# A two-layer network kernel whose instruction order is planned once, or planned in four passes ranked by latest begin

## The chip, the cores and the metric

The kernel runs on one core of one Trainium2 chip. The core has a matrix engine (TensorE, PE in the profile, with its weight loads as PEld), three engines for elementwise work (VectorE, DVE; ScalarE, ACT; GpSimd, POOL) and SyncE (SP), whose queue issues every transfer between device memory and the on-chip memory. The metric is the device time of one execution in microseconds (us). Each engine takes its instructions in the order in which the program lists them: an instruction that waits holds up all that stand behind it on its engine.

## The reference

All data are float32; x is 1024 tokens by 1024 features.

```python
for layer in range(2):
    h = rmsnorm(x, mix_norm[layer])
    # layer 0: sliding-window attention; layer 1: HGRN2 recurrence
    y = attention(h, ...) if layer % 2 == 0 else hgrn2(h, ...)
    x = x + y
    h = rmsnorm(x, mlp_norm[layer])
    x = x + square(relu(h @ w_up)) @ w_down          # 1024 -> 4096 -> 1024
return rmsnorm(x, final_norm)

def attention(h):    # 16 query heads, 4 key heads of 64, blocks of 128, window 128
    q, k, v = split(h @ w_qkv + b_qkv); q, k = rotary(q), rotary(k)
    scores = (q @ k.T) / 8, masked to the window, with a sink per head
    return (softmax with sink)(scores) @ v @ w_o

def hgrn2(h):        # 8 heads of 128, chunks of 64 tokens
    q, f, i, g = split(h @ w_in, 4)
    forget = lb + (1 - lb) * sigmoid(f); k = 1 - forget
    state = forget * state + outer(k, i); o = silu(q) @ state
    return (rmsnorm(o, g_norm) * silu(g)) @ w_o
```

## The kernel before

**Arithmetic.** Every float32 operand of a large product is split into a high part, rounded to the matrix engine's fast float32 form, and a low part, the remainder. A product is then three matmuls: high by high, high by low, low by high. For a weight block of 128x512 the high part is a cast (a tile named wh, on ACT or DVE) and the low part a subtraction on DVE (wl). The square products are done by Strassen's scheme, so weights and activations are also added and subtracted on DVE (tiles m and t) before they are split. The names after the letter are numbers of tiles: wr is a raw weight block as it is loaded, a and t are activations, sm are small columns of statistics, p and q are banks of PSUM, the matrix engine's accumulators (four of each), d are spills to device memory.

**Stages.** The tokens are worked in two halves of 512. In the profile the attention layer takes about 0 to 330 us, the first MLP 330 to 900, the recurrence 900 to 1400, the second MLP 1400 to 2070, the final norm the rest.

**What sets the order.** Nothing is issued when the model code runs. Each operation is recorded as an `Op` with the engines that may take it, a cost for each, and the tiles that it reads and writes (`Schedule.add`). Then `Schedule.order()` plays the whole list against a cost model: five engines, a latency from each engine to each other (`LATENCY`), a tail of 2750 ns behind every transfer, a `DRAIN` of 200 ns where the matmuls change between whole and column form, and for each sort of tile so many buffers (60 of a, 18 of t, 6 each of m and wr, 5 each of wh and wl, 4 each of p and q). Whenever an engine is free it takes, of the operations that are ready, the one of lowest rank. The rank is the place in the recorded program, less 100 for weight work (`LEAD`) and for what reads a p bank (`EVACUATE`). Buffers of a sort are given out in the order in which the program first uses them. `issue()` then emits the operations in the order found, so every instruction has the one line L337, that of the helper `issue` in `Net.call`, in the profile.

**What else is told apart there.** `copy` (casts and copies) and `square_relu` may go to ACT or DVE, and `better_elsewhere` decides by the waiting work of both. All loads and stores go through `dma` on SP.

Of the kernel before, what the change touches and what calls it, by code (L numbers as in the profile page):

```python
# [82 lines left out]
class Buf:  # L83
    def __init__(self, pool, bufs, shape, dtype, tag, name):
        self.pool, self.bufs, self.shape, self.dtype, self.tag, self.name = pool, bufs, shape, dtype, tag, name
        self.tile = None
        self.writer, self.readers = {}, {}
        self.uses, self.users = 0, []
        self.freed = 0.0
# [32 lines left out]
class Op:  # L122
    __slots__ = ("ways", "tail", "bufs", "first", "wait", "ready", "after", "rank", "engine", "form")
# [11 lines left out]
DRAIN = {"whole": 200.0, "columns": 200.0}  # L135
FULL = {512: 227.3, 256: 119.8}
# [6 lines left out]
class Schedule:  # L143
# [8 lines left out]
    def add(self, ways, outs, ins, tail=0.0, form=None):  # L152

        op = Op()
        op.ways, op.tail, op.engine, op.form = ways, tail, None, form
# [3 lines left out]
        op.rank, op.ready, op.after, op.first = (len(self.ops) - lead, len(self.ops)), 0.0, [], []  # L162
# [11 lines left out]
        op.bufs = list(bufs)  # L174
# [6 lines left out]
        op.wait = len(before) + len(op.bufs)  # L181
        for o in before:
            o.after.append(op)
        self.ops.append(op)

    def order(self):
        free_at, pending, ready, done, form = {}, {}, {}, [], None
        slots, queue = {}, {}
        for key, bufs in self.tags.items():
            slots[key] = [(0.0, k) for k in range(bufs[0].bufs)]  # L190
            queue[key] = list(reversed(bufs))

# [7 lines left out]
        def give(key):  # L200
            while queue[key] and slots[key]:
                b = queue[key].pop()
                t, b.slot = heapq.heappop(slots[key])
                for op in b.users:
                    met(op, t)

        for op in self.ops:
# [3 lines left out]
        for key in self.tags:  # L211
            give(key)
        def better_elsewhere(op, e, t):
# [8 lines left out]
        while True:  # L222
# [60 lines left out]
class Net:  # L283
# [48 lines left out]
    def op(self, engine, fn, outs, ins, cost, *args, tail=0.0, form=None, **kw):  # L332
        self.s.add({engine: self.call(fn, *args, **kw) + (cost,)}, outs, ins, tail, form)
# [13 lines left out]
    def dma(self, out, in_, nbytes):  # L347
        self.op("SP", self.nc.sync.dma_start, [out], [in_], max(450.0, nbytes / 320.0), out, in_, tail=2750.0)
# [7 lines left out]
    def act(self, out, in_, func, n=TH, bias=None, scale=1.0, accum=None):  # L356
# [6 lines left out]
        if accum is not None:  # L363
# [3 lines left out]
                out, in_, func, scale=scale, **kw)  # L367
# [1288 lines left out]
```

## Time and profile before

| what | value |
|---|---|
| median of 3 runs | 2086.56 us (2084.07 to 2086.97) |
| the profiled execution | 2086.78 us, of which the span from first to last instruction is 2084.9 us |
| mean granted TensorE clock | 0.997 |
| PE busy | 2062.8 us, 99% |
| DVE busy | 1893.6 us, 91% |
| ACT busy | 1122.4 us, 54% |
| transfers | 407.43 MB, mean 195 GB/s |

The busy time of PE comes from modelled ends, so two matmuls in a row may overlap in it. What the table leaves of PE, 2084.9 - 2062.8 = 22.1 us, is the time in which no matmul was under way. The rows that place these microseconds stand in the prediction.

### The profile page before, as it was taken

To read this page: it belongs to the slowest core of one execution; us is meant where nothing else is said; L and a number is where in the kernel's file an instruction comes from. 1 tells how busy PE (TensorE), PEld (TensorE's weight loads), DVE (VectorE), ACT (ScalarE), POOL (GpSimd) and SP (SyncE) were. 2 spreads that over 40 slices of the span, in tenths; PEclk is the share of its full clock that TensorE was granted. 3 is DMA by queue.
4 is the path that set the end of the run, shared out by engine and by line. 5 is a ranking of instruction groups with operands and counts; after the bars stand their busy time and mean duration, and the time that the engine had idled before them with its cause. 6 is when DMAs were issued, how large, how long until landed. Compare 5 with 4: busy or idle time off the path is not lost.

```text
span 2084.9 us, 35687 instructions
## 1 busy us (share of the span) xinstructions
PE 2062.8 (99%) x12220; PEld 1741.4 (84%) x12220; DVE 1893.6 (91%) x3919; ACT 1122.4 (54%) x2280; POOL 59.8 (3%) x121
## 2 busy tenths in 40 slices
PE   9999999999999999999999999999999999999998
PEld 7778888888898888887888888888788888888887
DVE  8889899999999989989898888888999999998995
ACT  5566777655565424556444444452765556432453
POOL 4030000000000000000000000000000000000000
PEclk9999999999999999999999999999999999999999
DMA  6212277867679967632222222567786768986732
GB/s 221 79 51 80 83 243 265 279 224 247 225 256 317 324 196 254 225 137 77 98 96 101 102 98 90 209 228 233 262 284 231 244 229 269 311 308 208 249 103 81
DMA packets 225845, 407.43 MB, mean 195 GB/s; under 512 B 25344, under 2 KB 30464, under 8 KB 225664
## 3 DMA queue, kind: packets, MB, share of 16 engines
q1 hardware_dynamic: 225664, 405.16, 57.1%
q8 instruction: 96, 1.57, 0.3%
q14 instruction: 85, 0.70, 0.1%
HBM read 321.17 MB, written 83.89 MB: 194 GB/s over the span
## 4 chain that ended last, share of the span: by engine, by line
PE 90%; DVE 5%; issue 2%; ACT 1%; DMA 1%; SPq 0%; POOLq 0%; POOL 0%; DVEq 0%; ACTq 0%
PE p L337 47%; PE q L337 43%; DVE t L337 2%; DVE a L337 2%; DVE wl L337 1%; ACT a L337 1%; DMA a<-d 0%; DVE m L337 0%; DMA a<-in_x 0%; ACT t L337 0%; DMA wr<-in_up 0%; ACT wh L337 0%; SPq L337 0%; ACT m L337 0%; DMA wr<-in_wo 0%
## 5 line engine op out<-in xcount | busy, mean ns | idle before, releaser
L337 PE MATMUL p<-a,wh 128*128 128x512 f32 (+1 forms) x2880 | 809.9, 365 | 0.8 <-ACT t L337 0.8
L337 PE MATMUL q<-a,wh 128*128 128x512 f32 x2112 | 655.0, 391 | 2.0 <-ACT t L337 1.9
L337 PEld LDWEIGHTS p<-a,wh 128*128 128x128 f32 x2880 | 514.5, 189 | 85.9 <-ACT t L337 2.1
L337 PE MATMUL p<-a,wl 128*128 128x512 f32 (+1 forms) x1440 | 520.7, 362 | 0.3 <-DVE wl L337 0.3
L337 PEld LDWEIGHTS q<-a,wh 128*128 128x128 f32 x2112 | 390.2, 188 | 79.0 <-ACT t L337 3.4
L337 PE MATMUL q<-a,wl 128*128 128x512 f32 x1056 | 410.9, 390 | 1.0 <-DVE wl L337 1.0
L337 PEld LDWEIGHTS p<-a,wl 128*128 128x128 f32 x1440 | 271.5, 189 | 40.7 <-DVE wl L337 0.8
L337 DVE TENSOR_TENSOR wl<-wr,wh 128x512 fp32r<-128x512 f32 x352 | 243.0, 692 | 7.9 <-ACT wh L337 3.3
L337 DVE TENSOR_TENSOR wl<-m,wh 128x512 fp32r<-128x512 f32 x338 | 232.0, 692 | 7.3
L337 ACT CAST wh<-wr 128x512 fp32r<-128x512 f32 x249 | 154.0, 619 | 150.5 <-PE p L337 107.2
L337 PEld LDWEIGHTS q<-a,wl 128*128 128x128 f32 x1056 | 198.7, 188 | 43.1 <-DVE wl L337 1.4
L337 ACT ACTIVATE t<-t 128x512 f32<-128x512 f32 x254 | 159.8, 632 | 111.2 <-DVE t L337 105.2
L337 ACT CAST wh<-m 128x512 fp32r<-128x512 f32 x240 | 149.1, 622 | 124.1 <-PE q L337 60.4
L337 DVE TENSOR_TENSOR a<-t,a 128x512 fp32r<-128x512 f32 (+2 forms) x314 | 208.4, 686 | 0.3 <-ACT t L337 0.3
L337 DVE TENSOR_TENSOR t<-t,t 128x512 f32<-128x512 f32 (+3 forms) x337 | 199.0, 607 | 3.7 <-ACT t L337 2.6
L337 ACT CAST a<-t 128x512 fp32r<-128x512 f32 (+1 forms) x212 | 127.0, 613 | 132.8 <-PE q L337 85.2
L337 ACT COPY t<-q 128x512 f32<-128x512 f32 (+2 forms) x201 | 112.5, 560 | 107.4 <-PE q L337 96.9
L337 PE MATMUL p<-wh,a 128*128 128x512 f32 x384 | 124.5, 396 | 1.1 <-DVE wl L337 1.1
L337 DVE TENSOR_TENSOR m<-wr,wr 128x512 f32<-128x512 f32 (+1 forms) x188 | 122.0, 652 | 2.5 <-DMA wr<-in_down 1.6
L337 DVE TENSOR_TENSOR t<-t,p 128x256 f32<-128x256 f32 x294 | 117.8, 420 | 0.0
L337 PEld LDWEIGHTS q<-t,t 128*64 128x64 f32 (+1 forms) x2160 | 95.5, 144 | 13.2 <-issue 7.3
L337 PE MATMUL q<-t,t 128*64 128x32 f32 (+2 forms) x2160 | 104.6, 229 | 0.0
(129 smaller groups left out, 2397.6 us busy)
## 6 DMA issues: line engine op xcount, KB each, us to landing
t<-d SPq DMA_DIRECT2D x548, 256.0 KB, 4.3
d<-t SPq DMA_DIRECT2D x244, 256.0 KB, 2.8
wr<-in_down SPq DMA_DIRECT2D x224, 256.0 KB, 4.2
wr<-in_up SPq DMA_DIRECT2D x178, 256.0 KB, 3.8
wr<-in_win SPq DMA_DIRECT2D x68, 256.0 KB, 2.6
a<-d SPq DMA_DIRECT2D x60, 256.0 KB, 4.5
wr<-in_wqkv SPq DMA_DIRECT2D x48, 256.0 KB, 2.6
d<-a SPq DMA_DIRECT2D x48, 256.0 KB, 3.8
```

The costliest lines, as they stand in the source:

```text
L337: fn(*[place(a) for a in args], **{k: place(v) for k, v in kw.items()})
```

## The change

The plan is made four times. `forward()` is the old `order()`, with a dearer cost model: loads have a tail of 3000 ns and stores of 2000, a change of the function table on ACT (Sqrt, Sin, Exp or Tanh after another) is charged 1283 ns, and ACT and DVE may not read one PSUM bank at the same time. Behind each plan `backward()` walks it from its end: for every operation it finds the latest begin that would still let everything behind it keep its time, given the engine it was put on and the buffers it was given. PE's operations stay in the planned order there and get no later than planned. In the next pass the rank of every operation that isn't PE's is this latest begin; PE's operations keep their program rank. The buffers of a sort are given out in the order of their first use in the plan just made. Of the four plans the one that ends first by the cost model is issued.

```diff
+LOAD, STORE = 3000.0, 2000.0
+READERS = {"ACT": "DVE", "DVE": "ACT"}
+TABLES = {AF.Sqrt: "sqrt", AF.Sin: "sin", AF.Exp: "exp", AF.Tanh: "exp"}
+TABLE, REUSE, PASSES = 1283.0, 200.0, 4
...
-    def order(self):
-        free_at, pending, ready, done, form = {}, {}, {}, [], None
+    def forward(self):
+
+        free_at, pending, ready, done, form, table = {}, {}, {}, [], None, None
...
         for key, bufs in self.tags.items():
-            slots[key] = [(0.0, k) for k in range(bufs[0].bufs)]
+            slots[key] = [(0.0, k, None) for k in range(bufs[0].bufs)]
             queue[key] = list(reversed(bufs))
+            for b in bufs:
+                b.uses, b.freed, b.read = len(b.users), 0.0, {}
...
+            if e in READERS:
+                held = max((b.read.get(READERS[e], 0.0) for b in op.banks), default=0.0)
+                if held > t + 1.0:
+                    heapq.heappush(p, (held, op.rank, op))
+                    continue
             op.engine, cost = e, op.ways[e][1]
+            for b in op.banks:
+                b.read[e] = t + cost + 130.0
             if op.form and op.form != form:
                 form, t = op.form, t + DRAIN[op.form]
-            free_at[e] = t + cost
-            end = t + cost + op.tail
+            if op.table and op.table != table:
+                table, t = op.table, t + TABLE
+            op.begin, free_at[e] = t, t + cost
+            op.end = end = t + cost + op.tail
...
-                    heapq.heappush(slots[key], (b.freed + 200.0, b.slot))
+                    heapq.heappush(slots[key], (b.freed + REUSE, b.slot, b))
...
+    def backward(self, done):
+        end = max(op.end for op in done)
+        place, heaps, free_at = {}, {e: [] for e in ENGINES}, dict.fromkeys(ENGINES, end)
+        for k, op in enumerate(done):
+            place[op], op.then, op.wait, op.late = k, [], 0, end
+        last = None
+        for op in done:
+            for o in op.before:
+                o.then.append((op, LATENCY[o.engine][op.engine]))
+            for b in op.first:
+                if b.previous:
+                    for o in b.previous.users:
+                        o.then.append((op, REUSE))
+            if op.engine == "PE":
+                if last:
+                    last.then.append((op, 0.0))
+                last = op
+        behind = {op: [] for op in done}
+        for op in done:
+            op.wait = len(op.then)
+            for o, gap in op.then:
+                behind[o].append((op, gap))
+        def push(op):
+            heapq.heappush(heaps[op.engine], (-op.late, -place[op], op))
+        for op in done:
+            if op.wait == 0:
+                push(op)
+        while any(heaps.values()):
+            e = max((e for e in ENGINES if heaps[e]), key=lambda e: min(free_at[e], heaps[e][0][2].late - heaps[e][0][2].tail))
+            _, _, op = heapq.heappop(heaps[e])
+            op.late = min(free_at[e], op.late - op.tail) - op.ways[e][1]
+            if e == "PE":
+                op.late = min(op.late, op.begin)
+            free_at[e] = op.late
+            for o, gap in behind[op]:
+                o.late = min(o.late, op.late - gap)
+                o.wait -= 1
+                if o.wait == 0:
+                    push(o)
+        for op in done:
+            if op.engine != "PE":
+                op.rank = (op.late, op.index)
+        for bufs in self.tags.values():
+            bufs.sort(key=lambda b: min(place[op] for op in b.users))
+    def order(self):
+        best = None
+        for k in range(PASSES):
+            done = self.forward()
+            end = max(op.end for op in done)
+            if best is None or end < best[0]:
+                best = (end, [(op, op.engine) for op in done], [(b, b.slot) for bufs in self.tags.values() for b in bufs])
+            self.backward(done)
+        for op, engine in best[1]:
+            op.engine = engine
+        for b, slot in best[2]:
+            b.slot = slot
+        return [op for op, _ in best[1]]
...
-        self.op("SP", self.nc.sync.dma_start, [out], [in_], max(450.0, nbytes / 320.0), out, in_, tail=2750.0)
+        self.op("SP", self.nc.sync.dma_start, [out], [in_], max(450.0, nbytes / 320.0), out, in_, tail=LOAD if isinstance(out, View) and out.buf.tag[0] != "d" else STORE)
...
-                out, in_, func, scale=scale, **kw)
+                out, in_, func, scale=scale, table=TABLES.get(func), **kw)
```

The recorded operations and the tiles are the same, and so is the number of instructions (10862 on PE, 1562 transfers). Only their order moves, and by the choice between ACT and DVE 6 casts and 5 of the squared relus go from ACT to DVE, all of 128x512. 9060 of PE's 10862 instructions stand at the same place as before. The helper's line is L416 in the changed program.

**VectorE in the attention layer (79 to 88 us in the trace of before).** a242 to a252 are query columns after the rotary step, which the first score products read. sm238 to sm240 are a norm's mean square, its root (which ACT makes) and the inverse root. Before:

```order
L337 TENSOR_SCALAR sm238_1154<-q237_1083 128x4
L337 SCALAR_TENSOR_TENSOR a242_1100<-q241_1090,a242_1100 64x512
L337 TENSOR_TENSOR a202_1092<-t203_1139,t204_1146 128x8x8
L337 RECIPROCAL sm239_1159<-sm239_1159 128x4
L337 SCALAR_TENSOR_TENSOR a243_1112<-q241_1090,a243_1112 64x512
L337 TENSOR_TENSOR sm240_1175<-sm239_1159 128x4
L337 SCALAR_TENSOR_TENSOR a245_1123<-q244_1097,a245_1123 64x512
L337 SCALAR_TENSOR_TENSOR sm240_1175<-sm238_1154,sm240_1175 128x4
L337 SCALAR_TENSOR_TENSOR a246_1132<-q244_1097,a246_1132 64x512
L337 SCALAR_TENSOR_TENSOR sm239_1159<-sm240_1175,sm239_1159 128x4
L337 SCALAR_TENSOR_TENSOR a248_1141<-q247_1106,a248_1141 64x512
L337 SCALAR_TENSOR_TENSOR a249_1149<-q247_1106,a249_1149 64x512
```
and now:

```order
L416 SCALAR_TENSOR_TENSOR a242_1100<-q241_1090,a242_1100 64x512
L416 SCALAR_TENSOR_TENSOR a243_1112<-q241_1090,a243_1112 64x512
L416 TENSOR_TENSOR a193_1069<-t194_1118,t195_1125 128x8x8
L416 SCALAR_TENSOR_TENSOR a245_1121<-q244_1097,a245_1121 64x512
L416 SCALAR_TENSOR_TENSOR a248_1132<-q247_1108,a248_1132 64x512
L416 SCALAR_TENSOR_TENSOR a246_1138<-q244_1097,a246_1138 64x512
L416 SCALAR_TENSOR_TENSOR a249_1142<-q247_1108,a249_1142 64x512
L416 SCALAR_TENSOR_TENSOR a251_1151<-q250_1115,a251_1151 64x512
L416 SCALAR_TENSOR_TENSOR a252_1157<-q250_1115,a252_1157 64x512
L416 COPY_PREDICATED m255_811<-c6364_68,c6566_71 128x2x128
L416 RECIPROCAL sm239_1163<-sm239_1163 128x4
L416 TENSOR_TENSOR wl307_1189<-wr305_998,wh306_1177 128x512
```
The RECIPROCAL, which needs the root from ACT, stood ahead of all but one of the query columns; now they all stand ahead of it.

**VectorE at the begin of the first MLP (338 to 345 us).** The t1021 rows are a running sum of squares, read by the column product q1029; m, wh and wl are weights of Strassen's scheme. Before:

```order
L337 TENSOR_TENSOR t1021_4097<-t1021_4097,t1023_4111 128x512
L337 TENSOR_TENSOR m1072_4363<-m1071_4342,wr1067_4100 128x512
L337 TENSOR_TENSOR t1021_4097<-t1021_4097,t1024_4176 128x512
L337 TENSOR_TENSOR m1073_4375<-wr1067_4100,wr1069_4158 128x512
L337 TENSOR_TENSOR t1021_4097<-t1021_4097,t1025_4205 128x512
L337 TENSOR_TENSOR m1074_4388<-wr1068_4132,m1072_4363 128x512
L337 TENSOR_TENSOR t1021_4097<-t1021_4097,t1026_4232 128x512
L337 TENSOR_TENSOR wl1076_4400<-m1071_4342,wh1075_4351 128x512
L337 TENSOR_TENSOR t1021_4097<-t1021_4097,t1027_4271 128x512
L337 TENSOR_TENSOR wl1078_4410<-m1072_4363,wh1077_4371 128x512
L337 TENSOR_TENSOR t1021_4097<-t1021_4097,t1028_4279 128x512
L337 TENSOR_TENSOR wl1080_4425<-m1074_4388,wh1079_4394 128x512
```
and now:

```order
L416 TENSOR_TENSOR t1017_3958<-t1017_3958,t970_3773 128x512
L416 TENSOR_TENSOR wl1056_4301<-m1047_4116,wh1055_4261 128x512
L416 TENSOR_TENSOR m1072_4310<-m1071_4256,wr1067_4122 128x512
L416 TENSOR_TENSOR t1021_4015<-t1021_4015,t1026_4119 128x512
L416 TENSOR_TENSOR a1002_4320<-t965_3849,a1001_4275 128x512
L416 TENSOR_TENSOR a1004_4328<-t969_3903,a1003_4299 128x512
L416 TENSOR_TENSOR t1021_4015<-t1021_4015,t1027_4184 128x512
L416 TENSOR_TENSOR t1013_3905<-t1013_3905,t966_3766 128x512
L416 TENSOR_TENSOR t1021_4015<-t1021_4015,t1028_4205 128x512
L416 TENSOR_TENSOR wl1058_4354<-wr1044_4079,wh1057_4291 128x512
L416 TENSOR_TENSOR a1011_4367<-t1009_3816,a1010_4103 128x512
L416 TENSOR_TENSOR wl1078_4372<-m1072_4310,wh1077_4356 128x512
```
The last sum (of t1028) stood behind wl1078 and now stands three rows ahead of it; m1073, m1074, wl1076 and wl1080, which stood around wl1078, have gone behind it, and it stands nine rows sooner (row 710, was 719).

**TensorE at the same place (344 us).** Before:

```order
L337 MATMUL q943_4150<-a1003_4290,wl1056_4295 128x512
L337 MATMUL q953_4221<-a989_3977,wh1077_4371 128x512
L337 MATMUL q953_4221<-a990_3993,wh1077_4371 128x512
L337 MATMUL q953_4221<-a989_3977,wl1078_4410 128x512
L337 MATMUL q953_4221<-a991_4053,wh1077_4371 128x512
L337 MATMUL q943_4150<-a1006_4140,wh1057_4297 128x512
L337 MATMUL q1029_4428<-c23_69,t1021_4097 128x1 x4
L337 MATMUL q943_4150<-a1007_4263,wh1057_4297 128x512
```
and now:

```order
L416 MATMUL q943_4159<-a1004_4328,wh1055_4261 128x512
L416 MATMUL q943_4159<-a1003_4299,wl1056_4301 128x512
L416 MATMUL q1085_4422<-a959_3822,wh1075_4325 128x512
L416 MATMUL q1085_4422<-a960_3853,wh1075_4325 128x512
L416 MATMUL q1085_4422<-a959_3822,wl1076_4392 128x512
L416 MATMUL q1085_4422<-a963_3841,wh1075_4325 128x512
L416 MATMUL q1085_4422<-a964_3859,wh1075_4325 128x512
L416 MATMUL q1085_4422<-a963_3841,wl1076_4392 128x512
```
The first product with wl1078 was row 1483; now q1085, which reads wl1076, stands there, and wl1078 is first read 25 rows later, at row 1508.

**ScalarE at 1472 to 1478 us, in the second MLP.** COPY t4199 empties bank q4198. In before 15 rows lie between it and COPY t4094, of which the last eleven stand here:

```order
L337 CAST a4142_17615<-t4108_17253 128x512
L337 ACTIVATE t4161_17623<-a4015_17145 128x512
L337 ACTIVATE t4163_17628<-a4035_17244 128x512
L337 CAST a4145_17634<-t4144_17437 128x512
L337 ACTIVATE t4164_17640<-a4045_17296 128x512
L337 ACTIVATE t4165_17646<-a4055_17361 128x512
L337 ACTIVATE t4166_17652<-a4065_17424 128x512
L337 CAST a4136_17657<-t4096_17111 128x512
L337 CAST a4149_17664<-t4148_17487 128x512
L337 ACTIVATE t4167_17671<-a4075_17490 128x512
L337 CAST wh4196_17676<-wr4183_17406 128x512
L337 COPY t4199_17682<-q4198_17611 128x512
```
Now, from COPY t4094 on:

```order
L416 COPY t4094_17616<-q4092_17552 128x512
L416 ACTIVATE t4084_17525<-t4084_17525 128x512 x2
L416 CAST wh4196_17632<-wr4183_17409 128x512
L416 ACTIVATE t4167_17641<-a4075_17501 128x512
L416 CAST wh4214_17658<-m4210_17650 128x512
L416 COPY t4199_17663<-q4198_17626 128x512
L416 CAST a4149_17672<-t4148_17380 128x512
```
Four rows (five instructions) are left between the two copies; most of the squares of a (t4160 to t4166) and the casts that stood there went ahead of the first copy or behind the second.

More of the change, by code (lines that the diff above doesn't have):

```diff
@@ L88, in __init__ @@
         self.uses, self.users = 0, []
[L89 removed]
+        self.freed, self.previous, self.read = 0.0, None, {}
     def keys(self, part):
@@ L122 @@
 class Op:
-    __slots__ = ("ways", "tail", "bufs", "first", "wait", "ready", "after", "rank", "engine", "form")
+    __slots__ = ("ways", "tail", "bufs", "first", "before", "after", "banks", "table", "rank", "form", "index",
+                 "wait", "ready", "engine", "begin", "end", "late", "then")
 ENGINES = ("SP", "PE", "ACT", "DVE", "Pool")
@@ L150, in tile, with add @@
         return View(Buf(pool, bufs, shape, dtype, tag, name))
-    def add(self, ways, outs, ins, tail=0.0, form=None):
+    def add(self, ways, outs, ins, tail=0.0, form=None, table=None):
         op = Op()
-        op.ways, op.tail, op.engine, op.form = ways, tail, None, form
+        op.ways, op.tail, op.form, op.table, op.index = ways, tail, form, table, len(self.ops)
         lead = self.lead
@@ L161, in add @@
             lead = max(lead, EVACUATE)
-        op.rank, op.ready, op.after, op.first = (len(self.ops) - lead, len(self.ops)), 0.0, [], []
+        op.rank, op.after, op.first = (len(self.ops) - lead, len(self.ops)), [], []
         before, bufs = set(), {}
@@ L173, in add @@
         before.discard(op)
-        op.bufs = list(bufs)
+        op.bufs, op.before = list(bufs), list(before)
+        op.banks = [v.buf for v in ins if isinstance(v, View) and v.buf.tag in "pq"]
         for b in op.bufs:
@@ L202, in give @@
                 b = queue[key].pop()
-                t, b.slot = heapq.heappop(slots[key])
+                t, b.slot, b.previous = heapq.heappop(slots[key])
                 for op in b.users:
                     met(op, t)
+        for op in self.ops:
+            op.wait, op.ready, op.engine = len(op.before) + len(op.bufs), 0.0, None
         for op in self.ops:
@@ L329, in psum, with op @@
         return self.tile(tag, BUFS[tag], (P, TH), F32, self.pp)
-    def op(self, engine, fn, outs, ins, cost, *args, tail=0.0, form=None, **kw):
-        self.s.add({engine: self.call(fn, *args, **kw) + (cost,)}, outs, ins, tail, form)
+    def op(self, engine, fn, outs, ins, cost, *args, tail=0.0, form=None, table=None, **kw):
+        self.s.add({engine: self.call(fn, *args, **kw) + (cost,)}, outs, ins, tail, form, table)
     def call(self, fn, *args, **kw):
```

1 line of the change is left out of this document (removed).

## The prediction

> **What bounds the kernel now.** I read the page's busy line first, then the stretches, then for whom TensorE waits, last the rows around each wait.
>
> ```profile
> PE 2062.8 (99%) x12220; PEld 1741.4 (84%) x12220; DVE 1893.6 (91%) x3919; ACT 1122.4 (54%) x2280; POOL 59.8 (3%) x121
> ```
>
> TensorE carries the time: 2062.8 of the span of 2084.9 us. The matmuls stay the same, so a new order can give back only what TensorE waits, at most 22.1 us. Where these are (window, its length, then busy us of PE, PEld, DVE, ACT, POOL, the granted clock, DMA share, GB/s):
>
> ```profile
> 0.00:100.00 100.00, 94.49 (x447) 77.48 (x448) 86.88 (x239) 56.91 (x125) 24.66 (x50) 1.00 0.45 153
> 100.00:200.00 100.00, 97.81 (x569) 76.33 (x567) 91.35 (x222) 64.06 (x209) 19.09 (x38) 1.00 0.17 59
> 200.00:300.00 100.00, 99.99 (x595) 79.84 (x594) 91.76 (x185) 74.74 (x239) 3.61 (x10) 1.00 0.43 146
> 300.00:400.00 100.00, 98.90 (x477) 82.77 (x476) 97.02 (x198) 69.78 (x126) 0.00 (x0) 0.98 0.80 271
> 340.00:350.00 10.00, 9.00 (x37) 7.12 (x36) 9.81 (x22) 3.51 (x7) 0.00 (x0) 0.83 0.80 269
> 400.00:900.00 500.00, 500.00 (x2583) 429.59 (x2582) 465.02 (x879) 261.30 (x445) 0.36 (x2) 1.00 0.74 250
> 900.00:1000.00 100.00, 98.82 (x600) 80.69 (x600) 93.80 (x208) 54.08 (x104) 0.54 (x2) 1.00 0.27 93
> 1000.00:1400.00 400.00, 398.62 (x3451) 334.99 (x3449) 349.55 (x801) 191.80 (x421) 7.70 (x17) 1.00 0.37 127
> 1400.00:1500.00 100.00, 98.14 (x447) 81.10 (x446) 91.87 (x178) 47.70 (x87) 0.00 (x0) 1.00 0.76 253
> 1500.00:2000.00 500.00, 500.00 (x2624) 431.06 (x2623) 469.61 (x904) 264.61 (x453) 0.00 (x0) 1.00 0.77 259
> 2000.00:2085.00 85.00, 76.01 (x447) 67.54 (x445) 56.79 (x116) 37.42 (x77) 3.86 (x3) 0.95 0.14 52
> ```
>
> The MLPs (400 to 900, 1500 to 2000) lose nothing, the last 85 us 8.99 and the first 100 us 5.51. In between lie the places that an order can mend: 2.19 us in 100 to 200, 1.10 in 300 to 400, 1.18 in 900 to 1000, 1.38 from there to 1400, 1.86 to 1500. VectorE is the only other engine near full. TensorE's largest waits (total us, times, longest):
>
> ```profile
> PE q L337 <- ACT t L337: 3.4, 4, 1.3
> PE q L337 <- DVE a L337: 2.6, 5, 1.6
> PE q L337 <- DVE t L337: 2.6, 4, 0.9
> PE p L337 <- DVE wl L337: 1.8, 3, 1.1
> ```
>
> They are for ACT and DVE, whose order the change replaces.
>
> **The change part by part.** The sum is made against the profiled execution, 2086.78 us, of which 1.9 lie around the span; it stands 0.22 above the median of 2086.56.
>
> *Attention.* TensorE's rows, then VectorE's, then ScalarE's:
>
> ```profile
> 40.11 0.44 PE L337 MATMUL q<-c,t 128*128 128x128 f32 x2 [0.85 <-DVE t L337]
> ...
> 83.09 0.35 PE L337 MATMUL q<-a,a 128*128 128x256 f32 x1 [1.56 <-DVE a L337]
> ```
> ```profile
> 82.04 0.18 DVE L337 RECIPROCAL sm<-sm 128x4 f32<-128x4 f32 x1 [1.85 <-ACT sm L337]
> 82.25 0.69 DVE L337 SCALAR_TENSOR_TENSOR a<-q,a 64x512 fp32r<-64x512 f32 x1
> ```
> ```profile
> 80.51 1.28 ACT L337 ACT_TABLE_LOAD   x1
> 81.80 0.20 ACT L337 ACTIVATE sm<-sm 128x4 f32<-128x4 f32 x1
> ```
>
> The RECIPROCAL heads VectorE's queue and waits 1.85 us for the root, which ScalarE makes behind a table load of 1.28. Behind it waits the row at 82.25 (a243); 0.15 us after that ends, TensorE goes on with the first score product. The new plan charges the table load and puts all query rows ahead of the RECIPROCAL. Late next: that product also moves eight rows forward on TensorE (319, was 327), some 8 x 0.23 = 1.8 us, so the wait goes only if a243 comes 1.56 + 1.8 = 3.4 us sooner. It stands sixteen rows sooner on VectorE, but part of what it passed is soon wanted too. I take -1.0 of 1.56 (0 to -1.56). At 40.11 the transposes wait 0.85 for t121; its last DVE row is 18 sooner (97, was 115), TensorE's 17 (123, was 140): -0.5 (0 to -0.85). From 100 to 200 the waits are many and short: -1.0 of 2.19 (0 to -2.19). The start (5.51 less 0.85 and 1.56 is 3.1 us) is the first loads: 0.
>
> *First MLP's begin.*
>
> ```profile
> 344.53 0.50 PE L337 MATMUL q<-a,wl 128*128 128x512 f32 x1 [1.00 <-DVE wl L337]
> ...
> 346.13 0.72 PE L337 MATMUL q<-a,wh 128*128 128x512 f32 x1
> ...
> 349.63 0.62 PE L337 MATMUL q<-a,wh 128*128 128x512 f32 x2
> 350.09 0.40 PE L337 MATMUL q<-a,wl 128*128 128x512 f32 x1
> ```
> ```profile
> 343.77 0.70 DVE L337 TENSOR_TENSOR wl<-m,wh 128x512 fp32r<-128x512 f32 x1
> 344.37 0.70 DVE L337 TENSOR_TENSOR t<-t,t 128x512 f32<-128x512 f32 x1
> ```
>
> TensorE waits 1.00 us for wl1078, made at 343.77 among sums that nobody reads before 345. Soon after it runs slow: the 8 matmuls from 346.13 to 349.63 take 0.437 us each, the two from 349.63 to 350.09 0.23; the window 340 to 350 has a clock of 0.83. That is 8 x 0.207 = 1.66 us, 2.66 with the wait. In the new order wl1078 stands nine rows sooner, 9 x 0.60 = 5.4 us by the step of these two rows, and is read 25 rows later. Late next is wl1076, now read in its place (row 1484, was 1500) and only three rows sooner on VectorE. I take -2.2 (0 to -2.66).
> The Trainium skill ("TensorE: Matmul & The Clock Gate", Part 1) says that the clock halves only after at least one idle window of some 3.4 us. By it this wait couldn't have cost the clock, the slow stretch would have another cause and stay, and the term would be -1.0 at most; the trace, whose 0.437 us steps begin 1.6 us behind the wait, speaks for the wait.
>
> *The recurrence.* Of 1.18 us in 900 to 1000 I take -0.7 (TensorE's products stand in whole groups of 12 there now, but VectorE is 93.8% busy), of 1.38 to 1400 -0.5 (each from 0 to the whole).
>
> *Second MLP.*
>
> ```profile
> 1469.47 0.58 ACT L337 COPY t<-q 128x512 f32<-128x512 f32 x1
> ...
> 1477.76 0.58 ACT L337 COPY t<-q 128x512 f32<-128x512 f32 x1
> ```
> ```profile
> 1478.39 0.73 PE L337 MATMUL q<-a,wh 128*128 128x512 f32 x2 [1.10 <-ACT t L337]
> ...
> 1485.34 0.50 PE L337 MATMUL q<-a,wh 128*128 128x512 f32 x1 [0.76 <-ACT t L337]
> ```
>
> The COPY at 1477.76 (t4199) empties the bank that TensorE takes at 1478.39. Fifteen instructions lie between the copies, 8.29 / 16 = 0.52 us each; five now, so it can begin 10 x 0.52 = 5.2 us sooner, against 1.10. TensorE's rows are the same, and the copy behind the wait at 1485.34 moves up too: -1.7 of 1.86 (0 to -1.86).
>
> *Moved work.* Six casts (0.43 us) and five squares (0.69, as the row at 82.25) go to DVE, 6.0 us:
>
> ```profile
> L337 DVE CAST wh<-wr 128x512 fp32r<-128x512 f32 x103 | 44.2, 429 | 39.1 <-PE p L337 23.6 <-PE q L337 12.6 <-DMA wr<-in_wqkv 2.6
> ```
>
> VectorE idles 191 us of the span, which hides it; all of it in 300 to 400, with 2.98 us idle, would cost 3.0. Late ranks can also leave VectorE idle early and full later; in attention that can cost what its pockets hold now, 2.59 + 2.90 = 5.5 us:
>
> ```profile
> 220.00:230.00 10.00, 10.00 (x72) 7.93 (x69) 7.41 (x17) 8.25 (x33) 0.22 (x1) 1.00 0.33 97
> 260.00:270.00 10.00, 10.00 (x71) 7.57 (x70) 7.10 (x16) 5.67 (x21) 0.00 (x0) 1.00 0.30 103
> ```
>
> New stalls are then 0 to 8.5; I take +1.2, near the lower end, since TensorE waits only 0.01 us in 200 to 300.
>
> *The end.* The order around the last 85 us is unchanged: 0.
>
> Sum: -0.5 - 1.0 - 1.0 - 2.2 - 0.7 - 0.5 - 1.7 + 1.2 = -6.4; 2086.78 - 6.4 = 2080.4 us, 0.30% below the median. All terms whole and no new stall: -(0.85 + 1.56 + 2.19 + 2.66 + 1.18 + 1.38 + 1.86) = -11.7, 2075.1; some 24 waits also break the overlap of two matmuls (0.40 long at a step of 0.23), 0.17 each, 4.1 more: 2071.
>
> **The rivals.** *Absorbed, within 0.2%.* The waits go, and as much comes back where VectorE is fullest: -7.6 + 5.5 to + 8.5, 2084.7 to 2087.7. For it: the 97.02, and ranks that by their making leave no slack. With it goes the case that little changes, since TensorE keeps its rank and 9060 of 10862 places.
>
> *Slower: loads come too late.* The plan counts a load of 256 KB at 0.82 us of issue and 3.0 of tail, 3.82. Medians from issue to landing:
>
> ```profile
> t<-d SPq DMA_DIRECT2D x548, 256.0 KB, 4.3
> ...
> wr<-in_down SPq DMA_DIRECT2D x224, 256.0 KB, 4.2
> ```
>
> A load ranked by its latest begin lands up to 0.48 us behind the plan. The MLPs' 1000 us, at 12 x 0.23 = 2.75 us for a product, are 364 products; each that finds an operand late loses up to 0.48. From (6.4 + 4.2) / 0.48 = 22 such the kernel is slower by over 0.2%; 31 give 2080.4 + 15 = 2095. Against it: the plan before counted 0.25 less and waits nowhere there, and raw weights are fetched when one of their six buffers comes free, whatever the rank.
>
> *The clock's slow stretch stays.* The wait at 344.53 goes, but TensorE runs slow from 346 all the same, for a reason that the order doesn't touch. Against it: no other window from 400 to 2000 has a clock below 1.00. With its 1.66 us back in the sum, 2082.1. By the Trainium skill's rule above this would come.
>
> **How the numbers follow.** 0.2% (4.2 us) is about what a measurement here can tell from no change: faster is below 2082.4, slower above 2090.7. Forecast 0.52 and the clock's rival 0.10, both faster: 0.62. Absorbed or idle 0.19, late loads 0.19. The forecast's own range is 2071 to 2084; with the late loads it reaches to 2095, which leaves out some 0.12.
>
> **What would show it.** Right: no wait of VectorE for the root ahead of the score products; TensorE 99.8 or more from 300 to 400 at a clock of 1.00; no wait at the copies near 1478; the MLPs still at 500.00. Wrong: TensorE waits for wl1076, or for a load in 330 to 900 or 1500 to 2000; VectorE idle up to 150 us and waited for from 225 to 300; a second stretch below a clock of 1.00.

## The result, and the profile after

The changed kernel takes 2077.79 us (median of 6 runs, 2077.14 to 2078.63) against 2085.78 us for the kernel before (6 runs): a ratio of 0.9962, 95% interval 0.9949 to 0.9975. The forecast was 2080.4 us with a range of 2071 to 2095. The profiled execution has a span of 2076.9 us, 8.0 less than before.

The busy line and the stretches of the changed kernel (window, its length, busy us of PE, PEld, DVE, ACT, POOL, clock, DMA share, GB/s):

```profile
PE 2058.8 (99%) x12220; PEld 1746.1 (84%) x12220; DVE 1894.4 (91%) x3929; ACT 1109.9 (53%) x2265; POOL 58.2 (3%) x121
```
```profile
0.00:100.00 100.00, 93.81 (x426) 76.72 (x427) 83.31 (x229) 54.22 (x117) 23.55 (x50) 0.98 0.46 151
100.00:200.00 100.00, 97.98 (x562) 78.32 (x561) 91.79 (x221) 65.00 (x216) 18.68 (x38) 1.00 0.18 56
300.00:400.00 100.00, 100.00 (x492) 84.82 (x491) 97.36 (x190) 66.34 (x119) 0.00 (x0) 1.00 0.84 273
340.00:350.00 10.00, 10.00 (x50) 8.38 (x49) 9.63 (x19) 6.45 (x13) 0.00 (x0) 1.00 0.74 225
400.00:900.00 500.00, 500.00 (x2584) 429.79 (x2584) 468.21 (x907) 256.48 (x438) 0.36 (x2) 1.00 0.76 250
900.00:1000.00 100.00, 100.00 (x625) 83.43 (x624) 94.13 (x198) 55.46 (x108) 0.61 (x2) 1.00 0.28 91
1000.00:1400.00 400.00, 399.79 (x3444) 338.26 (x3443) 352.96 (x811) 189.71 (x418) 7.61 (x16) 1.00 0.39 132
1400.00:1500.00 100.00, 100.00 (x458) 83.10 (x457) 91.94 (x175) 56.22 (x101) 0.00 (x0) 1.00 0.78 256
1500.00:2000.00 500.00, 500.00 (x2626) 431.60 (x2625) 470.18 (x907) 258.08 (x444) 0.00 (x0) 1.00 0.77 254
```

From 300 to 2000 us TensorE now idles 0.21 us; before it idled 5.52. The first 200 us idle 8.21, before 7.70. One new wait makes up half of that. TensorE's largest waits in the changed kernel, then the rows at that wait, of TensorE and of VectorE:

```profile
PE p L416 <- DVE a L416: 4.1, 2, 3.9
PE q L416 <- ACT t L416: 1.8, 3, 1.3
PE q L416 <- DVE sm L416: 1.4, 1, 1.4
```
```profile
53.76 0.39 PE L416 MATMUL p<-wh,a 128*128 128x512 f32 x1
58.05 0.47 PE L416 MATMUL p<-wh,a 128*128 128x512 f32 x1 [3.90 <-DVE a L416]
...
59.95 1.05 PE L416 MATMUL p<-wh,a 128*128 128x512 f32 x2
60.80 0.63 PE L416 MATMUL p<-wl,a 128*128 128x512 f32 x1
```
```profile
49.73 1.19 DVE L416 TENSOR_TENSOR t<-q,a 64x128 fp32r<-64x128 f32 x4
...
54.17 0.68 DVE L416 TENSOR_TENSOR t<-t,t 128x512 f32<-128x512 f32 x1
54.78 0.68 DVE L416 TENSOR_TENSOR wl<-wr,wh 128x512 fp32r<-128x512 f32 x1
55.38 1.40 DVE L416 SCALAR_TENSOR_TENSOR a<-a,c,a 128x512 fp32r<-128x512 f32 x2
56.70 0.41 DVE L416 TENSOR_TENSOR a<-a 128x256 f32<-128x256 f32 x1
57.15 2.73 DVE L416 SCALAR_TENSOR_TENSOR a<-p,sm,a 128x512 f32<-128x512 f32 x4
```

VectorE does not idle there. It works off sums of squares (t<-t,t) and other rows that TensorE does not wait for there, and reaches the row that empties TensorE's bank (57.15) only when TensorE has stood for 3.2 us (from 53.76 + 0.23). Then TensorE runs at steps of 0.43 us for a while: the ten matmuls from 58.05 to 61.99 take 3.94 us, 1.64 more than at 0.23.

To set the stages beside each other I use one measure more, worked out from the begins of TensorE's rows in the trace: for the matmuls of 512 and 256 columns, the step from one's begin to the next matmul's, less the dense step (0.230 us for 512 columns, 0.122 for 256), added up where it is over. It holds waits, half-speed steps and broken overlap.

| lost over the dense step, us | 0 to 300 | 300 to 2000 | the end | sum |
|---|---|---|---|---|
| before | 28.0 | 27.8 | 0.4 | 56.2 |
| after | 30.9 | 16.4 | 0.4 | 47.7 |

Attention became 2.9 us worse, the rest 11.4 us better; together 8.5, against 8.0 of the span.

### The profile page after: what moved, and what is told of

It reads as the page before. It is cut to its first block, busy times and chain, and to the rows that moved or that the text cites. A ratio compares the mean times of both kernels' runs of the same rounds, so it can differ in the third digit from the quotient of the medians.

```text
span 2076.9 us, 35708 instructions
## 1 busy us (share of the span) xinstructions
PE 2058.8 (99%) x12220; PEld 1746.1 (84%) x12220; DVE 1894.4 (91%) x3929; ACT 1109.9 (53%) x2265; POOL 58.2 (3%) x121
## 4 chain that ended last, share of the span: by engine, by line
PE 96%; DVE 2%; issue 1%; ACT 1%; DMA 0%; POOL 0%; POOLq 0%; SPq 0%; ACTq 0%; DVEq 0%
PE p L416 51%; PE q L416 44%; DVE a L416 1%; DVE t L416 1%; ACT a L416 1%; DVE wl L416 0%; ACT t L416 0%; DMA wr<-in_wqkv 0%; DVE m L416 0%; ACT wh L416 0%; POOL a L416 0%; POOLq L1709 0%; SPq L416 0%; ACT m L416 0%; DVE sm L416 0%
## 5 line engine op out<-in xcount | busy, mean ns | idle before, releaser
L416 PE MATMUL p<-a,wh 128*128 128x512 f32 (+1 forms) x2880 | 806.3, 364 | 0.0
L416 PE MATMUL q<-a,wh 128*128 128x512 f32 x2112 | 653.2, 391 | 0.0
L416 PEld LDWEIGHTS p<-a,wh 128*128 128x128 f32 x2880 | 515.2, 189 | 83.1 <-issue 0.4
L416 PE MATMUL p<-a,wl 128*128 128x512 f32 (+1 forms) x1440 | 522.2, 363 | 0.0
L416 PEld LDWEIGHTS q<-a,wh 128*128 128x128 f32 x2112 | 389.7, 188 | 75.3
L416 PE MATMUL q<-a,wl 128*128 128x512 f32 x1056 | 410.6, 389 | 0.0
L416 PEld LDWEIGHTS p<-a,wl 128*128 128x128 f32 x1440 | 271.9, 189 | 40.0
L416 ACT CAST wh<-wr 128x512 fp32r<-128x512 f32 x252 | 155.8, 620 | 186.3 <-PE p L416 117.5
L416 DVE TENSOR_TENSOR wl<-wr,wh 128x512 fp32r<-128x512 f32 x352 | 240.6, 688 | 6.3 <-ACT wh L416 2.5
L416 DVE TENSOR_TENSOR wl<-m,wh 128x512 fp32r<-128x512 f32 x338 | 231.6, 686 | 11.1 <-ACT wh L416 5.8
L416 ACT CAST wh<-m 128x512 fp32r<-128x512 f32 x252 | 155.8, 620 | 154.1 <-PE q L416 88.7
L416 PEld LDWEIGHTS q<-a,wl 128*128 128x128 f32 x1056 | 198.4, 188 | 42.0
L416 ACT ACTIVATE t<-t 128x512 f32<-128x512 f32 x244 | 153.8, 632 | 113.6 <-DVE t L416 107.8
L416 DVE TENSOR_TENSOR a<-t,a 128x512 fp32r<-128x512 f32 (+2 forms) x314 | 207.3, 678 | 6.6 <-PE q L416 5.5
L416 DVE TENSOR_TENSOR t<-t,t 128x512 f32<-128x512 f32 (+3 forms) x337 | 196.8, 599 | 5.7 <-ACT t L416 4.5
L416 ACT COPY t<-q 128x512 f32<-128x512 f32 (+2 forms) x201 | 111.4, 559 | 97.8 <-PE q L416 84.7
L416 ACT CAST a<-t 128x512 fp32r<-128x512 f32 (+1 forms) x199 | 119.2, 611 | 66.3 <-PE q L416 40.3
L416 PE MATMUL p<-wh,a 128*128 128x512 f32 x384 | 127.6, 403 | 5.1 <-DVE a L416 4.1
L416 DVE TENSOR_TENSOR m<-wr,wr 128x512 f32<-128x512 f32 (+1 forms) x188 | 121.4, 646 | 3.3 <-DMA wr<-in_down 1.5
L416 DVE TENSOR_TENSOR t<-t,p 128x256 f32<-128x256 f32 x294 | 118.6, 414 | 0.0
L416 PEld LDWEIGHTS q<-t,t 128*64 128x64 f32 (+1 forms) x2160 | 95.9, 144 | 12.9 <-issue 8.1
L416 PE MATMUL q<-t,t 128*64 128x32 f32 (+2 forms) x2160 | 104.8, 229 | 0.2 <-ACT t L416 0.2
```

The costliest lines, as they stand in the source:

```text
L416: fn(*[place(a) for a in args], **{k: place(v) for k, v in kw.items()})
```

## The experiments

Each was timed against the kernel before on its own chip; ratios are to that. All compute the whole reference, but for the clock probe (e5), which has a table of its own. The first table has every other run, with TensorE's idle time (window less busy) from the one execution of each kernel that was traced. That execution need not be the median one: e4's took 2075.4 us and e7's 2067.9, each the shortest of its four.

| kernel | median us (n) | ratio, 95% | PE idle 0 to 300 | PE idle 300 to 2000 |
|---|---|---|---|---|
| before | 2085.8 to 2087.6 | 1 | 7.71 | 5.52 |
| changed kernel | 2077.8 (6) | 0.9962 (0.9949 to 0.9975) | 8.41 | 0.21 |
| e1, one pass, new costs | 2080.2 (5) | 0.9967 (0.9954 to 0.9980) | 5.87 | 3.09 |
| e2, four passes, old costs | 2082.0 (7) | 0.9972 (0.9961 to 0.9983) | 9.56 | 1.85 |
| e3, one duration right | 2074.8 (4) | 0.9941 (0.9924 to 0.9957) | 6.47 | 0.21 |
| e4, VectorE 4% slower in the plan | 2079.4 (4) | 0.9959 (0.9944 to 0.9973) | 5.13 | 2.17 |
| e6, attention's durations right | 2070.4 (4) | 0.9921 (0.9906 to 0.9936) | 2.51 | 2.52 |
| e7, three more right | 2070.7 (4) | 0.9925 (0.9909 to 0.9942) | 3.84 | 0.37 |
| e8, one pass, load and store times only | 2086.2 (10) | 1.0000 (0.9991 to 1.0010) | 6.58 | 6.09 |
| e9, one pass, bank rule only | 2083.8 (10) | 0.9986 (0.9977 to 0.9995) | 7.61 | 4.32 |
| e10, one pass, table loads only | 2081.5 (10) | 0.9976 (0.9966 to 0.9985) | 5.90 | 4.00 |
| e11, one pass, e7's durations | 2081.7 (8) | 0.9977 (0.9967 to 0.9988) | 2.99 | 9.16 |

Two things need no run: with one pass and the old costs the planner gives the order of before, instruction for instruction, and with two passes that of the changed kernel; passes three and four end later by the plan and are dropped.

**The ranks or the costs? e1 and e2.** Theory A was that the ranks brought the gain, rival B that the new cost model did.

```diff
 # e1
-TABLE, REUSE, PASSES = 1283.0, 200.0, 4
+TABLE, REUSE, PASSES = 1283.0, 200.0, 1
 # e2
-LOAD, STORE = 3000.0, 2000.0
-READERS = {"ACT": "DVE", "DVE": "ACT"}
-TABLES = {AF.Sqrt: "sqrt", AF.Sin: "sin", AF.Exp: "exp", AF.Tanh: "exp"}
+LOAD, STORE = 2750.0, 2750.0
+READERS = {}
+TABLES = {}
```

> The dearer cost model alone: one forward pass, program ranks (PASSES = 1). Theory A, the ranks by latest begin brought the gain: the time stays within 0.2% of before, 2083 to 2089 us, and TensorE still waits about 1 us each near 344, 946 and 1478 us. Rival B, the cost model brought it (table load charged, loads 3.0 us, no two readers of a bank): 2081 us or less, and those waits are gone.

> The ranks by latest begin alone: four passes, but every transfer with a tail of 2750 ns, no table loads charged and no rule on two readers of a bank. Theory A: 2075 to 2081 us, TensorE at 500.00 of 500 in both MLPs and no wait over 0.5 us from 300 to 2000 us; the VectorE wait for the root behind the table load at 80 us may come back (1 to 2 us). Rival B: 2083 us or more.

Neither held alone: either half brings most of the gain, 0.33% and 0.28%, and both together 0.38%. (The three intervals overlap, so the times do not rank the three kernels; e2 lies between the ranges of both theories.) The windows 0 to 300 and 300 to 2000 of e1, of e2 and of the changed kernel:

```profile
0.00:300.00 300.00, 294.13 (x1610) 235.02 (x1611) 270.85 (x641) 200.56 (x579) 48.17 (x98) 1.00 0.37 121
300.00:2000.00 1700.00, 1696.91 (x10197) 1445.80 (x10197) 1571.62 (x3172) 889.53 (x1632) 8.54 (x20) 1.00 0.65 216
```
```profile
0.00:300.00 300.00, 290.44 (x1590) 233.58 (x1591) 268.38 (x640) 197.37 (x578) 44.00 (x98) 0.99 0.38 124
300.00:2000.00 1700.00, 1698.15 (x10205) 1447.12 (x10204) 1571.96 (x3171) 888.27 (x1631) 8.28 (x20) 1.00 0.64 215
```
```profile
0.00:300.00 300.00, 291.59 (x1594) 234.63 (x1595) 269.89 (x645) 195.48 (x574) 45.81 (x98) 0.99 0.37 122
300.00:2000.00 1700.00, 1699.79 (x10220) 1451.01 (x10219) 1574.78 (x3182) 882.28 (x1625) 8.58 (x20) 1.00 0.65 216
```

They work in different stages. The costs alone help attention (5.87 us idle, before 7.71) and leave 3.09 us behind it, where the waits for ScalarE's copies stay, as the rows of e1 show:

```profile
1470.64 0.73 PE L416 MATMUL q<-a,wh 128*128 128x512 f32 x2 [1.29 <-ACT t L416]
...
1477.50 0.73 PE L416 MATMUL q<-a,wh 128*128 128x512 f32 x2 [0.67 <-ACT t L416]
```

The ranks alone take out two thirds of the later waits (1.85 left) and make attention worse (9.56). In the changed kernel the ranks' loss in attention hides most of what the costs bring there.

**Which cost? e8, e9, e10.** One pass with one part of the cost model each: `LOAD, STORE`, `READERS` or `TABLES` as new, the other two as old. For e8:

```diff
-READERS = {"ACT": "DVE", "DVE": "ACT"}
-TABLES = {AF.Sqrt: "sqrt", AF.Sin: "sin", AF.Exp: "exp", AF.Tanh: "exp"}
-TABLE, REUSE, PASSES = 1283.0, 200.0, 4
+READERS = {}
+TABLES = {}
+TABLE, REUSE, PASSES = 1283.0, 200.0, 1
```

> The plan of before (one pass, program ranks) with one part of the new cost model: loads 3000 ns, stores 2000. If this part brought what one pass with the whole new cost model gained (7.4 us, e1), 2079 to 2082 us without the wait at 344 us; if it is one of the other two, 2085 to 2089 us with that wait still there.

> The plan of before with the rule alone that VectorE and ScalarE are not planned to read one PSUM bank at once. If this part brought the gain of e1, 2079 to 2082 us, the waits of attention shorter; if not, 2085 to 2089 us.

> The plan of before with the table loads alone charged (1283 ns). By its order a243 stands ahead of the RECIPROCAL at 80 us, so the wait of 1.56 us there falls below 0.5 us; elsewhere only what follows from that: 2084 to 2087 us. If it brought the gain of e1, 2079 to 2082 us.

The load times show no effect (1.0000). The bank rule brings 0.14%, between its two forecasts, the table loads 0.24%; the sum, 0.38%, is e1's 0.33% within the intervals. In e10 the first score product (at 83.09 us before) no longer waits, its row carries no wait; a later one, at 84.42, waits 0.59 us for another cause:

```profile
81.80 0.28 PE L416 MATMUL q<-a,a 128*128 128x256 f32 x1
81.91 0.40 PE L416 MATMUL p<-wh,a 128*128 128x512 f32 x1
```

This is more than e10's expectation gave it (2084 to 2087 us): what moves at 80 us moves the order behind it too.

**Why the new wait at 54 us? e3, e4, e6, e7.** The changed kernel's own plan has VectorE's row of 57.15 begin at 49.57 us, 7.6 sooner; TensorE is 2.9 us behind its plan there. Theory C: VectorE is behind its plan because some durations in it are too short, and the plan had filled what looked like idle time ahead of that row with work that could wait. Rival D: ranks without slack make such a wait whatever the durations. e3 put one duration right, the low part of the keys (203 ns in the plan; the four at 49.73 take 1.19 us, 0.30 each):

```diff
-        cost = {"DVE": 70 + n * 1.04, "Pool": 147 + n * 2.105}
+        cost = {"DVE": 70 + n * 1.04 + 92 * (n == P and x.buf.tag in "pq"), "Pool": 147 + n * 2.105}
```

> The changed kernel with one duration put right in the plan: the 64x128 subtraction from PSUM on VectorE (low part of the keys) is charged 295 ns as the trace has it, not 203. Theory C, the new 3.9 us wait at 54 us comes from VectorE being behind its plan by then (28 such rows x 0.09 = 2.6 us of it): the wait shrinks to about 1.3 us, the half-speed stretch behind it goes, 2073 to 2076 us. Rival D, the wait comes from ranks without slack, whatever the durations: it stays at 3 to 4 us, 2077 to 2079 us.

It took 2074.8 us, in theory C's range. The wait went from 3.90 to 2.71 us, neither to 1.3 nor unmoved, and in the traced execution the half-speed steps behind it are gone (steps of 0.23 from 56.64 on):

```profile
56.33 0.47 PE L416 MATMUL p<-wh,a 128*128 128x512 f32 x1 [2.71 <-DVE a L416]
56.64 0.40 PE L416 MATMUL p<-wl,a 128*128 128x512 f32 x1
56.87 0.63 PE L416 MATMUL p<-wh,a 128*128 128x512 f32 x2
```

e4 makes every VectorE duration 4% longer in the plan:

```diff
-            op.engine, cost = e, op.ways[e][1]
+            op.engine, cost = e, op.ways[e][1] * (1.04 if e == "DVE" else 1.0)
```

> The changed kernel with every VectorE duration 4% longer in the plan, so that VectorE is rather ahead of its plan than behind it. Theory C: at 54 us VectorE has 4% of 50 = 2 us more in hand, the wait falls to 2 us or less, and attention waits less: 2072 to 2077 us. Rival D: the wait stays, and longer durations only shift other work: 2077 to 2082 us.

The wait near 54 us fell to 0.67, as theory C has it, and attention idles 5.13 us instead of 8.41; but 2.17 us come back from 300 to 2000. The time, 2079.4 us, lies in rival D's range and not in C's. e6 puts right what the traces show wrong in attention, ScalarE's part too:

```diff
+                self.s.extra = 126
                 self.copy(dst, src, P)
+                self.s.extra = 92
                 self.tt("DVE", kl[g][r, c].only(n), src, dst.bitcast(F32), ALU.subtract, P)
...
+                    self.s.extra = 137
                     self.act(s[r], pq[r], AF.Copy, scale=HD**-0.5)
+                    self.s.extra = 112
                     self.stt(s[o], pq[r], HD**-0.5, s[r].bitcast(F32), ALU.mult, ALU.subtract)
```

(extra is added to the planned cost of the operations listed right below it, and is 0 otherwise.)

> The changed kernel with four durations of the attention stage put right in the plan, each as the trace has it: ScalarE's 64x128 key casts 285 ns (159 planned), VectorE's 64x128 subtractions 295 (203), ScalarE's 64x512 query copies 616 (479), VectorE's 64x512 query remainders 714 (602). Theory C, VectorE and ScalarE behind their plan make the attention waits: the wait at 54 us falls below 1 us, TensorE is busy 295 us or more of the first 300 (291.6 in the changed kernel), 2069 to 2074 us. Rival D, the ranks leave no slack whatever the durations: a wait of 2 to 4 us stays or comes up elsewhere in attention, 2074 to 2079 us.

It took 2070.4 us. The wait at 54 us is gone; these are all waits of TensorE in its first 300 us, and the window:

```profile
PE p L417 <- DVE t L417: 1.0, 1, 1.0
PE p L417 <- ACT a L417: 1.0, 1, 1.0
PE p L417 <- DVE wl L417: 0.3, 1, 0.3
PE q L417 <- DVE m L417: 0.2, 1, 0.2
```
```profile
0.00:300.00 300.00, 297.49 (x1640) 242.67 (x1641) 274.49 (x652) 200.89 (x586) 48.80 (x98) 1.00 0.40 131
```

So theory C holds as far as these runs go: as the durations come nearer to the trace, the wait goes from 3.90 to 2.71 to nothing, with the same rule for the ranks. (Each plan also orders other places anew, so the times carry more than this one wait, and e4 shows that a shorter wait there does not by itself make the kernel faster.) e7 puts three of the later stages right as well:

```diff
+            self.s.extra = 130
             self.copy(s[:CH, :, 0].only(1), scores[:CH, c], 4 * CH)
             self.copy(s[CH:, :, 1].only(2), scores[CH:, c], 4 * CH)
             self.copy(s[:CH, :, 1].only(3), cross[:, c], 4 * CH)
...
-[target], [mask, part], 70 + TH // 2 * 1.04, target
+[target], [mask, part], 258 + TH // 2 * 1.04, target
...
-(on_act, 2 * (94 + TH * 0.834))
+(on_act, 2 * (174 + TH * 0.834))
```

> As the attention durations put right, and three more of the later stages: ScalarE's 64x4x64 copies 130 ns dearer, the masked copies of the recurrence 188, the pair of squared relu 160. Theory C: attention as in the kernel with the attention durations alone, and 1 to 2 us less waiting from 900 to 1400 us, 2068 to 2073 us. Rival D: no gain on it, 2073 to 2079 us.

It took 2070.7 us, no other time than e6's. Two waits for ScalarE that e6 has behind 300 us (near 398 and 1530) are gone, 0.37 us of idle time is left instead of 2.52, and attention has 1.3 us more. That the three durations gained 1 to 2 us from 900 to 1400 did not show: there was nothing left to gain (0.21 us idle there in e6 already).

**Are right durations enough? e11.** e7's durations with one pass and program ranks.

```diff
-TABLE, REUSE, PASSES = 1283.0, 200.0, 4
+TABLE, REUSE, PASSES = 1283.0, 200.0, 1
```

> The measured durations of e7 with one pass and program ranks. Theory A, ranks by latest begin are worth most of the gain from 300 us on whatever the durations: 2074 to 2081 us, waits of about 1 us back near 942, 1470 and 1478 us. Rival: right durations alone do it, 2072 us or less.

2081.7 us, 0.7 above theory A's range and far from the rival's: attention is as good as in e7 (2.99 us idle), but 9.16 us are idle behind it, with waits at 941, 1470 and 1477 us and others as long or longer at 339, 364 and 1503. With durations that are right the ranks are worth about 11 us (0.9925 against 0.9977, intervals apart); with the durations as they came the same step, e1 to the changed kernel, is 0.9967 to 0.9962, which the intervals do not tell from nothing.

**What costs the clock? e5.** A kernel with nothing but bursts of dense matmuls and waits of set length between them, all of it four times.

```diff
+    for turn in range(4):
+        for n in (-1, 0, 1, 2, 3, 4, 6):        # length of the VectorE chain TensorE waits for
+            y, z = pause(ps, n)
+            ps = burst(32 + turn, y)
+        for n in (4, 8, 12):                    # one-column matmuls behind a short wait
+            y, z = pause(ps, -1)
+            columns(z, n)
+            ps = burst(32 + turn, y)
```

> Not the network: only bursts of 32 to 35 dense 128x512 matmuls (7.3 to 8 us), between which TensorE waits for a chain of VectorE instructions, about 1.0, 1.4, 2.0, 2.6, 3.2, 3.8 and 5.0 us, and three bursts that follow a wait of some 1.0 us with 4, 8 or 12 one-column matmuls in it; all of it four times. The outputs are a test tile. Theory E, as the prediction read the trace: a plain wait of about 1 us costs the clock, so 0.43 us steps follow the short waits too. Rival F, the Trainium skill's rule: only waits of some 3.4 us or more are followed by 0.43 us steps, none of the shorter ones, with or without columns. Rival G: a short wait costs the clock only where one-column matmuls follow it, as at 344 us in the kernel before.

| idle time of TensorE between bursts, us | bursts with 0.43 us steps |
|---|---|
| 1.24 (two lengths alike) | 0 of 8 |
| 1.97 (once 2.06) | 1 of 4 |
| 2.69 | 0 of 4 |
| 3.42 | 4 of 4 |
| 4.14 and 5.60 | 8 of 8 |
| 0.78 (once 0.86), then 4 one-column products | 0 of 4 |
| 0.78, then 8 | 2 of 4 |
| 0.78, then 12 | 4 of 4 |

Two of the bursts:

```profile
49.65 7.55 PE L416 MATMUL p<-a,wh 128*128 128x512 f32 x32 [2.69 <-DVE a L416]
60.62 9.14 PE L416 MATMUL p<-a,wh 128*128 128x512 f32 x32 [3.42 <-DVE a L416]
```

The same 32 matmuls take 7.55 us behind 2.69 us of idle time and 9.14 behind 3.42. Theory E falls: a plain wait of 1.24 us never cost the clock. Rival F, the rule of the Trainium skill ("TensorE: Matmul & The Clock Gate", Part 1: the clock halves after at least one idle window of some 3.4 us), agrees where the wait was 3.42 us or more. As a bound on the length of a wait it does not hold, and the measurement decides: one burst in four at 1.97 us was slow, and so are the steps behind a plain wait of 1.90 us in e2 and of 1.84 us in e11. Rival G holds for 12 one-column products and for half of the bursts with 8.

What decides shows in the clock column of the windows. In the probe the clock changes only on a grid of 3.413 us (61.82, 65.24, 72.06, 78.89 us and so on), and a stretch at half clock is one or two whole windows of that grid (the last one ends with the trace). I took the grid of each of the 13 traces from its own changes of the clock and counted, in every window at full clock, the time without a matmul, one-column products counted as idle. All 34 windows with 1.90 us or more were followed by half clock, none of the 7319 with 1.62 or less, and two of the seven between (1.65 to 1.87). So about half a window is enough, and where a wait lies on the grid counts. The changed kernel, e2 and e3, each window with the next:

```profile
55.06:58.47 3.41, 0.42 (x2) 0.41 (x3) 3.38 (x6) 0.00 (x0) 0.00 (x0) 1.00 0.25 77
58.47:61.88 3.41, 3.41 (x10) 2.63 (x9) 3.41 (x11) 0.00 (x0) 0.00 (x0) 0.50 0.08 22
```
```profile
53.74:57.15 3.41, 1.51 (x7) 0.99 (x6) 3.38 (x7) 0.62 (x1) 0.00 (x0) 1.00 0.23 77
57.15:60.56 3.41, 3.41 (x9) 2.66 (x9) 3.41 (x9) 0.00 (x0) 0.00 (x0) 0.50 0.04 6
```
```profile
51.08:54.49 3.41, 2.54 (x12) 1.76 (x10) 3.28 (x9) 1.73 (x4) 2.70 (x7) 1.00 0.29 99
54.49:57.90 3.41, 1.57 (x7) 1.33 (x8) 3.38 (x6) 0.00 (x0) 0.00 (x0) 1.00 0.13 48
57.90:61.32 3.42, 3.42 (x17) 2.83 (x16) 3.42 (x14) 0.62 (x1) 0.00 (x0) 1.00 0.30 89
```

In e2 the whole 1.90 us lie in one window; in e3 a border at 54.49 cuts the 2.71 us into 0.88 and 1.84. A wait of 3.90 us leaves 1.95 or more in one window wherever it lies, so by these counts it always costs the clock; that e3's wait did not was the luck of its place.

## Why the prediction was right, and where not

The direction, the range and the place of nearly every gain were right: -8.0 us against -6.4. That the sum came so near is in part luck: the new stalls were 4.7 us dearer than taken, and some 4 us of gain stood in no term. By its own terms, in TensorE's idle time and slow steps:

| term | taken | measured |
|---|---|---|
| 40 us | -0.5 | -0.85, no wait left |
| 83 us | -1.0 | -1.56, no wait left |
| 100 to 200 us | -1.0 | -0.17 (2.02 left of 2.19) |
| first MLP's begin, with the slow steps | -2.2 | -2.66 |
| 900 to 1000 | -0.7 | -1.18 |
| 1000 to 1400 | -0.5 | -1.17 |
| 1400 to 1500 | -1.7 | -1.86 |
| start, and what is short up to 100 us | 0 | -0.8 (3.10 to 2.29) |
| the last 100 us | 0 | +0.5 |
| new stalls | +1.2 | +5.9: 4.29 - 0.23 at 54 us, 1.64 of slow steps, 0.2 from 200 to 300 |

The measured column comes to -3.9; the other 4.1 us of the 8.0 are in neither. Part is overlap: the list of waits before has 24, after 14, at 0.17 each 1.7 us. The prediction priced that only for its lower bound, though it belongs to every wait that goes. The remaining 2.4 us lie in steps a little longer than dense without any idle time; which of them, no figure here says.

**The term that failed is the new stalls.** It was mis-sized, 1.2 for 5.9, within its bound of 8.5, and it was looked for in the wrong place: the prediction took the thin cover to lie from 220 to 300 us and in 300 to 400, after VectorE's idle pockets and its 97%. It came at 54 us, in a stretch where TensorE waited nowhere before, and with it one of the prediction's own signs of being wrong, a second stretch below a clock of 1.00. The slow steps there (1.64 us) undid the gain of those at 346 us (1.66). What the prediction did not do is compare the plan's durations with the trace, row by row: a plan that fills every gap is as good as its durations there, and attention's were 92 to 137 ns short in four sorts of row. The late-load rival, which did look at a duration of the plan, had the wrong one: charging loads more changed nothing (e8), and the changed kernel's MLPs stayed at 500.00.

**"The wait cost the clock" was right for the traced execution, but not for the wait alone.** In e8 the same wait is longer, with the same column products behind it, and the clock stays at 1.00:

```profile
344.60 0.51 PE L416 MATMUL q<-a,wl 128*128 128x512 f32 x1 [1.27 <-DVE wl L416]
...
345.41 0.94 PE L416 MATMUL q<-c,t 128*128 128x1 f32 x8
```

The windows of the grid tell the two apart, first before, then e8:

```profile
342.79:346.20 3.41, 2.41 (x16) 1.82 (x14) 3.41 (x6) 1.10 (x2) 0.00 (x0) 1.00 0.82 280
346.20:349.61 3.41, 3.41 (x9) 2.66 (x9) 3.38 (x11) 1.47 (x3) 0.00 (x0) 0.50 0.76 282
```
```profile
340.40:343.82 3.42, 2.93 (x13) 2.08 (x12) 3.42 (x6) 1.59 (x3) 0.00 (x0) 1.00 0.91 299
343.82:347.23 3.41, 2.63 (x15) 2.32 (x16) 3.37 (x9) 0.28 (x3) 0.00 (x0) 1.00 0.87 302
347.23:350.64 3.41, 3.41 (x16) 2.82 (x15) 3.41 (x11) 3.02 (x6) 0.00 (x0) 1.00 0.78 252
```

Before, one window holds the whole wait of 1.00 us and 0.65 us of column products, 1.65 together, and the next runs at half clock; it is the least that any window ahead of a slow one held. In e8 a border at 343.82 leaves 1.43 in the fuller window. Windows with 0.65 us of column products and no wait, which every trace of the network has, never cost the clock. So the 2.66 us went as forecast, with the step as the prediction had it; that the 1.66 of it stood in the profile to be gained was the luck of the grid, and whether the other executions of before had it, no trace shows. The prediction's rival on it would have been 2082.1.

**The credit was given to the ranks.** The prediction names the table charge once, at 83 us, and takes the rest as the ranks' work. e1 and e10 show that the cost model alone is worth 0.33%, the table loads 0.24% of it. At 1478 us the prediction's step holds: that wait stays in e1 and goes with the ranks.

The rivals absorbed and slower did not come about, though attention by itself is slower: without the gains behind 300 us the change would have cost about 3 us.

## What to carry to other kernels

A list plan that ranks by latest begin fills every gap in front of work that is not ready yet, so a duration that is 0.1 us short in a row that is issued dozens of times turns into a wait of the bound engine; before changing the ranks, compare the plan's begin of each instruction with the trace and mend the durations that drift. Here the new costs, the ranks and right durations together gave 0.75 to 0.79%, the change as it came 0.38%, the costs and right durations without the ranks 0.23%. And read a planner's change in parts, stage by stage: a sum of -8 us can be -11 in one stage and +3 in another, and the +3 is the next thing to mend.

## What was not expected of the hardware

The clock is granted in windows of 3.413 us on a grid of its own, and about half a window without dense matmuls was enough to halve the next: a wait of 1.84 or 1.90 us did it where it lay in one window, one of 2.71 did not where a border cut it. One-column matmuls do not keep the clock up: 0.78 us of idle time and 12 such products, together some 3.5 us, halved it 4 times of 4, as 3.42 us of plain waiting did, and 8 of them 2 times of 4.

On VectorE and ScalarE the rows on 64 partitions that read PSUM take 92 to 137 ns more from one begin to the next than the plan's formula gives: 0.295 us for the 64x128 subtraction (0.203), 0.714 for the 64x512 remainder (0.602), 0.616 for the 64x512 copy on ScalarE (0.479), 0.285 for its 64x128 cast (0.159). Their busy time is no longer than that of 128 partitions (before: 0.288 us for the 64x128 subtraction and for a 128x128 row t<-a,c alike). What is missing is the overlap: VectorE's rows of 128x512 are 0.69 us long and begin 0.60 apart, while the 64x512 remainders are 0.69 long and begin 0.71 to 0.72 apart. Whether the 64 partitions or the order of reads from one bank takes it away, no run separates.
